# A hybrid decoder step on one core: the down projection's first 3584 rows as seven block products

## The chip, the cores and the metric

The kernel runs on one core of a Trainium2 chip. Its time is the device time of one execution in microseconds (us), and the number to predict is the median over runs. The engines are TensorE (PE, matmuls into PSUM), VectorE (DVE), ScalarE (ACT), GpSimd (POOL, which works on SBUF) and SyncE (SP, which here only issues DMAs). Each has its own queue of instructions that it takes in order; semaphores tie the queues together.

## The reference

1088 tokens (1024 of a prompt, 8 x 8 of samples), width 1024, one layer:

```python
h = rmsnorm(x, g_attn[i])
q, k, v, z, b_raw, a_raw, p, ga, gb = jnp.split(h @ w_in[i], offs, axis=-1)
...                                   # gated delta rule -> o_a; causal pooling -> o_b
merged = jax.nn.sigmoid(ga) * (o_a @ w_a_out[i]) + jax.nn.sigmoid(gb) * (o_b @ w_b_out[i])
x = x + merged @ w_o[i]
h2 = rmsnorm(x, g_mlp[i])
x = x + jnp.square(jax.nn.relu(h2 @ w_up[i])) @ w_down[i]
...
y = rmsnorm(x, g_final)
```

w_up is 1024 x 4096 and w_down 4096 x 1024. The rest of the outputs (states) are written before the part that the change touches. All is float32.

## The kernel before

**Layout and products.** Activations stand with channels on the 128 partitions and the 1088 tokens along the free axis (NT); a weight block of 128 x 128 is the stationary side of a matmul, tokens are the moving side. To keep float32 accuracy on a faster matmul type every operand is split into a hi part (a rounded copy, made by ACT) and a lo part (the rest, a subtraction of two SBUF tiles on DVE): `split`, lines 1045 and 1046. A product is three matmuls: hi x hi, hi x lo, lo x hi (lines 145 to 147, 1207).

**The stages around the change, in order.** `outs` merges the branches into tiles `mg`. `project(c)` runs for the two halves c of the tokens (CT = 544, each again cut in CB = 272): it multiplies by w_o, adds x, writes the new x (called x1) to DRAM (`x1_d`), sums squares into `acc` (ACT squares, POOL adds, L1126), and builds the seven token side operands of Strassen's algorithm for the up projection (`F`, L1132), split into `B[c]`. `norm2` turns `acc` into one over the norm: matmuls with ones (L1149), an inverse root on DVE (L89 to L94), transposes on PE (L82), a copy to `rb`. For c = 0 it is called in the second block of `project(1)`, for c = 1 after the first product of the up projection.

**The up projection** (`up_all`, `up_pair`) takes 16 pairs of 128 channels of w_up. A pair has seven products q (`product`, L1207), each 2 token halves x 4 blocks of depth x 3 matmuls of 272 columns, that is 168 matmuls. The weight operands of the next pair (`a_op`: sums on DVE into `S`, then a split) are made between the products, their loads (`a_raw`, L1169) a pair ahead. The products gather in three PSUM tiles b1, b2, b3 (out of four, `pp`): ACT copies partial sums out to SBUF (`copied`, L1224), DVE adds them (`plus`, L1236), `done` applies relu and the norm (DVE, L1230) and squares (ACT, L1231), and SP stores the result to DRAM (`h_d`, L1232).

**The down projection** (`down_all`) takes 8 groups of 512 rows of w_down. For 7 of them it loads h back (`acts`, L1287), splits it, and for each of 8 blocks of output channels and three stretches of tokens (384, 384, 320) makes 4 x 3 matmuls (`gemm`) into one PSUM tile, which DVE adds into x1 in SBUF (L1310). That is 288 matmuls a group. Weights are loaded and split per two output blocks (`weights`, L133, L134). The eighth group is done in `finish` with the tokens on partitions, together with the transposes of x1, the last norm and the output.

**Order.** The program text gives a priority; the scheduler of the tile framework lays out each engine's queue from it by a simulation, with tile slots handed out as they come free, and inserts the semaphores. A pool opened on memory that an older pool held makes its tiles wait for the older tiles that they overlap (`reuse_waits="tile"`). A tile of a ring (`big`, `bigy`, `tmp`, `wh`) waits in the same way for its predecessor's last reader.

Of the kernel before, what the change touches and what calls it, by code (L numbers as in the profile page):

```python
# [18 lines left out]
P = 128  # L19
# [50 lines left out]
class Builder:  # L70
    def __init__(self, tc, a, o):
        self.tc, self.nc, self.a, self.o = tc, tc.nc, a, o
        self.n, self.turn = 0, {}
# [129 lines left out]
    def build(self):  # L203
        tc, nc = self.tc, self.nc
        with ExitStack() as ctx, ExitStack() as ctx2:
# [12 lines left out]
            self.h_d = self.dp.tile([FF // P, P, NT], F32, name="h_d")  # L218
# [54 lines left out]
            ctxx.close()  # L273
            ctxy.close()
            self.pm = ctx.enter_context(tc.tile_pool(name="pm2", bufs=1, space=PSUM, reuse_waits="tile"))
            self.X = ctx.enter_context(tc.tile_pool(name="D", bufs=1, reuse_waits="tile"))
            self.nbig, self.mx = 27, self.X
            self.down_all()
# [4 lines left out]
    def bigy(self, dt=F32):  # L283
        return self.Y.tile([P, NT], dt, name=self.name("bigy"), tag="bigy", bufs=18)
# [778 lines left out]
    def outs(self):  # L1063
        nc, v = self.nc, self.nc.vector
        self.mg = [[tuple(self.bigy(F32R).rearrange("p (m t) -> p m t", m=2) for _ in range(2)) for _ in range(4)]
                   for _ in range(2)]
# [26 lines left out]
    def project(self, c):  # L1093
# [3 lines left out]
        ops = [tuple((self.big if c == 0 or q < 2 else self.bigy)(F32R).rearrange("p (k t) -> p k t", k=4)  # L1097
                     for _ in range(2)) for q in range(7)]
        self.B.append(ops)
        acc = self.st.tile([P, CT], F32, name=self.name("acc"), tag="acc", bufs=1)  # L1100
        cols = slice(c * CT, (c + 1) * CT)
        for i in range(KD):
# [10 lines left out]
            if i == 1 and c == 1:  # L1113
                self.norm2(0, self.acc)
# [24 lines left out]
        self.acc = acc  # L1139

    def norm2(self, c, acc):

        nc, v = self.nc, self.nc.vector
        ss = self.sm.tile([P, 6], F32, name=self.name("ss2"), tag="ms6", bufs=2)
        v.memset(ss, 1.0)
        ps = self.pp()[:, 0, :]
        cuts = [(b, j, min(P, CB - j * P)) for b in range(2) for j in range(3)]
        for n, (b, j, rows) in enumerate(cuts):
            nc.tensor.matmul(ps[0:rows, n:n + 1], lhsT=acc[:, b * CB + j * P:b * CB + j * P + rows],  # L1149
                             rhs=self.one, start=True, stop=True)  # L1150
        for n, (b, j, rows) in enumerate(cuts):
            v.tensor_scalar(out=ss[0:rows, n:n + 1], in0=ps[0:rows, n:n + 1], scalar1=1.0 / D, scalar2=EPS,
                            op0=ALU.mult, op1=ALU.add)
        rstd = self.rsqrt(ss, 6)
        ps = self.pp()
        for n, (b, j, rows) in enumerate(cuts):
            self.tr(ps[:, b, j * P:j * P + rows], rstd[0:rows, n:n + 1].broadcast_to([rows, P]), rows)
        nc.scalar.copy(out=self.halves(self.rb[:, c * CT:(c + 1) * CT]), in_=ps[:, :, 0:CB])


    def a_raw(self, i):

        if not hasattr(self, "raws"):
            self.raws, self.aops, self.ss_, self.na = {}, {}, {}, -1
        if i < 16 and i not in self.raws:
            tag = ("wr", "wl")[i % 2]
            self.raws[i] = [self.wp.tile([P, 4, 256], F32, name=self.name("raw"), tag=tag, bufs=2) for _ in range(2)]
            for j, t in enumerate(self.raws[i]):
                self.nc.sync.dma_start(out=t, in_=self.a["w_up"][0, j * 512:(j + 1) * 512, i * 256:(i + 1) * 256]  # L1169
                                       .rearrange("(k p) c -> p k c", p=P))  # L1170

    def a_op(self, i, q):
# [18 lines left out]
        self.na += 1  # L1191
        if self.na % 5 == 4:
            t = self.wp.tile([P, D], F32R, name=self.name("ao"), tag="wh", bufs=2)
        else:
            t = self.bigy(F32R)
# [14 lines left out]
    def up_pair(self, i, cs, side):  # L1210
# [11 lines left out]
        def copied(ps):  # L1222
            t = self.tmp()
            nc.scalar.copy(out=at(t), in_=ps[:, sl, 0:CB])  # L1224
            return t

        def done(src, t, row, n):

            rb = self.rb.rearrange("p (c n t) -> p n c t", c=2, n=2)[:, n, sl, :]
            v.scalar_tensor_tensor(out=at(t), in0=src, scalar=0.0, in1=rb, op0=ALU.max, op1=ALU.mult)  # L1230
            nc.scalar.activation(out=at(t), in_=at(t), func=AF.Square)  # L1231
            nc.sync.dma_start(out=self.h_d[2 * i + row].rearrange("p (c n t) -> p n c t", c=2, n=2)[:, n, sl, :],  # L1232
                              in_=at(t))
# [5 lines left out]
        c1 = copied(b1)  # L1239
# [18 lines left out]
        done(at(c16), c16, 0, 1)  # L1258
        side(5)
        run(6, b1, False)  # L1260
        h21 = self.tmp()
        done(b1[:, sl, 0:CB], h21, 1, 0)
        side(6)

    def up_all(self):
        def first(q):
            if q + 2 < 7:
                self.a_op(0, q + 2)
            if q == 0:
                self.norm2(1, self.acc)  # L1270
                self.a_raw(1)
        self.up_pair(0, (0,), first)
        self.up_pair(0, (1,), lambda q: self.a_op(1, q))
        for i in range(1, 16):
            def side(q):
                if q == 0:
                    self.a_raw(i + 1)
                self.a_op(i + 1, q)
            self.a_raw(i + 1)
# [3 lines left out]
    def acts(self, g):  # L1283
        out = []
        for f in range(4 * g, 4 * g + 4):
            raw = self.big()
            self.nc.sync.dma_start(out=raw, in_=self.h_d[f])  # L1287
            hi, lo = self.big(F32R), self.big(F32R)
            for n in range(2):
                s = slice(n * CT, (n + 1) * CT)  # L1290
                self.split(hi[:, s], lo[:, s], raw[:, s])
            out.append((hi, lo))
            yield out

    def down_all(self):
        v = self.nc.vector
        *_, acts = self.acts(0)
        self.x1 = []
        for m in range(KD):
            self.x1.append(self.big())  # L1300
            self.nc.sync.dma_start(out=self.x1[m], in_=self.x1_d[m])
        for g in range(7):
            nxt = self.acts(g + 1)
            for m in range(KD):
                if m % 2 == 0:
                    w = self.weights(self.a["w_down"][0, g * 512:(g + 1) * 512, m * P:(m + 2) * P], 4)
                for tb, (t0, n) in enumerate(TBS):
                    ps = self.gemm(w, m % 2, self.sub(acts), tb, 4)
                    x = self.x1[m][:, t0:t0 + n]
                    v.tensor_tensor(out=x, in0=x, in1=ps, op=ALU.add)  # L1310
                if m % 2 == 1:
                    new = next(nxt)
            acts = new
        self.finish(acts, 7 * 512)

    def finish(self, acts, row):
# [3 lines left out]
        for k in range(4):  # L1320
            raw = self.load(self.a["w_down"][0, row + k * P:row + (k + 1) * P, :], 1)
            hi, lo = (self.big(F32R), self.big(F32R)) if k < 4 - 3 else (None, None)
            w.append(self.weights(None, 1, raw=raw, hi=hi, lo=lo))
        gf = self.X.tile([P, D], F32, name="gf", tag="gf", bufs=1)
        nc.gpsimd.dma_start(out=gf, in_=self.a["g_final"].unsqueeze(0).broadcast_to([P, D]))
        xn = [self.X.tile([P, 3, D], F32, name=self.name("xn"), tag=t, bufs=1) for t in ("hi0", "lo0", "hi1")]
        for c in range(NCH):
            rows = P if c < 8 else 64
            tok = slice(c * P, c * P + rows)
            y = xn[c // 3][0:rows, c % 3, :]  # L1330
# [6 lines left out]
            for s in range(2):  # L1337
# [9 lines left out]
                junk = self.X.tile([P, 512], BF16, name=self.name("jf"), tag="lo2", bufs=1)  # L1347
# [35 lines left out]
```

## Time and profile before

| | |
|---|---|
| median of 3 runs | 1586.9 us (1586.44 to 1590.38) |
| profiled execution | 1586.38 us, span of its instructions 1584.6 us |
| mean granted TensorE clock | 0.985 of full |
| PE busy | 1532.2 us (97%), 10443 matmul records |
| DVE, ACT, POOL busy | 942.9, 520.1, 95.9 us |
| DMA | 171.16 MB, 108 GB/s over the span |

Times in the profile count from the first instruction. A busy time is the sum of an engine's instructions, overlaps counted once. Matmuls overlap each other, so the length of one matmul record (about 0.29 us for 272 columns) is more than the step from one to the next; paces have to be taken from events that repeat. "idle ... <-X" names what the engine waited for. [...]

### The profile page before, as it was taken

How to read it: one execution, taken by the hardware profiler on the slowest of the kernel's cores; microseconds unless marked ns; L12 is line 12 of the kernel's file. 1: busy time of each engine (PE TensorE's matmuls, PEld its weight loads, DVE VectorE, ACT ScalarE, POOL GpSimd, SP SyncE). 2: the span in 40 equal slices, each digit the busy share in tenths (PEclk: the TensorE clock that was granted, in tenths of full speed). 3: DMA queues.
4: the chain of work that ended last, by engine and by line, in shares of the span. 5: the costliest groups of instructions: out<-in, count | busy, mean ns of one | idle time of the engine just before them, and what ended most of it. 6: DMA issues, size and time to landing. Idle time of an engine off the chain costs nothing. (4 is left out here: it accounts for less than half of the span.)

```text
span 1584.6 us, 26354 instructions
## 1 busy us (share of the span) xinstructions
PE 1532.2 (97%) x10443; PEld 1485.2 (94%) x10443; DVE 942.9 (60%) x2197; ACT 520.1 (33%) x1103; POOL 95.9 (6%) x129
## 2 busy tenths in 40 slices
PE   6999999999999999999889999999989999999997
PEld 5989898998999999999889999999979999999986
DVE  7677768758664274656676555555545454444456
ACT  5342423413322133214454444444432222111123
POOL 3200000000000122002220000000000000000000
PEclk9999999999999999999898999999989999999999
DMA  6431422232223434444443333332255323222212
GB/s 221 137 98 49 117 77 71 90 90 72 79 86 105 129 88 138 137 132 157 145 151 103 103 110 110 103 101 93 83 184 202 108 97 101 92 69 96 82 41 74
DMA packets 173541, 171.16 MB, mean 108 GB/s; under 512 B 19924, under 2 KB 155837, under 8 KB 173409
## 3 DMA queue, kind: packets, MB, share of 16 engines
q1 hardware_dynamic: 168137, 157.24, 31.3%
q0 software_dynamic: 4080, 12.13, 2.3%
q8 instruction: 82, 1.34, 0.4%
q14 instruction: 42, 0.34, 0.1%
q10 hardware_dynamic: 1200, 0.10, 0.1%
HBM read 118.73 MB, written 50.83 MB: 107 GB/s over the span
## 5 line engine op out<-in xcount | busy, mean ns | idle before, releaser
L145 PE MATMUL pm<-big,wh 128*128 128x384 f32 (+1 forms) x864 | 283.4, 329 | 6.9 <-ACT big L1045 6.9
L145 PE MATMUL pm<-hi,wh 128*128 128x384 f32 (+1 forms) x840 | 284.3, 339 | 0.1
L146 PE MATMUL pm<-lo,wh 128*128 128x384 f32 (+1 forms) x840 | 282.4, 336 | 1.3 <-DVE lo L425 1.3
L147 PE MATMUL pm<-big,wl 128*128 128x384 f32 (+1 forms) x864 | 283.6, 328 | 0.0
L146 PE MATMUL pm<-big,wh 128*128 128x384 f32 (+1 forms) x864 | 283.4, 328 | 0.0
L147 PE MATMUL pm<-hi,wl 128*128 128x384 f32 (+1 forms) x840 | 280.4, 334 | 0.0
L1207 PE MATMUL pp<-big,bigy 128*128 128x272 f32 x1392 | 189.4, 291 | 2.8 <-ACT bigy L1045 2.8
L133 ACT CAST wh<-wr 128x1024 fp32r<-128x1024 f32 x88 | 92.5, 1051 | 294.4 <-PE pm L146 241.5
L1207 PEld LDWEIGHTS pp<-big,bigy 128*128 128x128 f32 x1392 | 182.2, 192 | 3.2 <-ACT bigy L1045 2.9
L1310 DVE TENSOR_TENSOR big<-big,pm 128x384 f32<-128x384 f32 x168 | 88.9, 531 | 151.7 <-PE pm L147 151.7
L145 PEld LDWEIGHTS pm<-big,wh 128*128 128x128 f32 x864 | 163.1, 189 | 8.3 <-ACT big L1045 8.0
L147 PEld LDWEIGHTS pm<-big,wl 128*128 128x128 f32 x864 | 163.2, 189 | 0.0
L146 PEld LDWEIGHTS pm<-big,wh 128*128 128x128 f32 x864 | 163.1, 189 | 0.0
L146 PEld LDWEIGHTS pm<-lo,wh 128*128 128x128 f32 x840 | 159.6, 190 | 3.6 <-DVE lo L425 1.8
L145 PEld LDWEIGHTS pm<-hi,wh 128*128 128x128 f32 x840 | 159.2, 190 | 2.5 <-DVE hi L421 0.5
L147 PEld LDWEIGHTS pm<-hi,wl 128*128 128x128 f32 x840 | 159.5, 190 | 0.2
L134 DVE TENSOR_TENSOR wl<-wr,wh 128x1024 fp32r<-128x1024 f32 x88 | 107.7, 1224 | 65.7 <-ACT wh L133 62.4
L1207 PE MATMUL pp<-bigy,bigy 128*128 128x272 f32 x768 | 106.8, 288 | 0.0
L1207 PEld LDWEIGHTS pp<-bigy,bigy 128*128 128x128 f32 x768 | 100.3, 188 | 0.0
L147 PE MATMUL pp<-bigy,wl 128*128 128x272 f32 x256 | 74.6, 291 | 0.0
L145 PE MATMUL pp<-bigy,wh 128*128 128x272 f32 x256 | 74.4, 291 | 0.0
L146 PE MATMUL pp<-bigy,wh 128*128 128x272 f32 x256 | 74.2, 290 | 0.0
(341 smaller groups left out, 2256.0 us busy)
## 6 DMA issues: line engine op xcount, KB each, us to landing
big<-h_d SPq DMA_DIRECT2D x32, 544.0 KB
wr<-in_w_in_dram SPq DMA_DIRECT2D x33, 512.0 KB
raw<-in_w_up_dram SPq DMA_DIRECT2D x32, 512.0 KB
wr<-in_w_down_dram SPq DMA_DIRECT2D x32, 512.0 KB
h_d<-tmp SPq DMA_DIRECT2D x60, 272.0 KB
wr<-in_w_o_dram SPq DMA_DIRECT2D x16, 512.0 KB
tmp<-xT_d SPq DMA_DIRECT2D x16, 272.0 KB
x_d<-tmp POOLq DMA_DIRECT2D x16, 272.0 KB, 2.3
```

The source lines that it names most:

```text
L133: nc.scalar.copy(out=hi, in_=raw)
L134: (nc.gpsimd if early else nc.vector).tensor_tensor(out=lo, in0=raw, in1=hi.bitcast(F32), op=ALU.subtract)
L145: mm(ps, lhsT=wh, rhs=xh, start=first, stop=False)
L146: mm(ps, lhsT=wh, rhs=xl, start=False, stop=False)
L147: mm(ps, lhsT=wl, rhs=xh, start=False, stop=last)
L1207: mm(out, lhsT=l[:, k, :], rhs=r[:, k, :], start=first and k + n == 0, stop=k == 3 and n == 2, skip_group_check=not first)
L1310: v.tensor_tensor(out=x, in0=x, in1=ps, op=ALU.add)
```

## The change

The down projection of rows 0 to 3583 is made by the same algorithm of seven products. Seven token side operands per pair of up channels are stored (`F_d`) in place of h: three are results of `done` themselves, four are differences that POOL makes in the up projection (`less`). In the down projection each group of 512 rows has four steps (two token halves c, two halves pp of the output channels); a step has seven products of 2 x 2 x 3 matmuls of 272 columns. The weight side sums are made by POOL (`da_op`), x1 (`x1t`) is loaded by ACT's queue, and additions into x1 are shared by DVE (straight from PSUM) and POOL (from ACT's copies). The PSUM pool of the up projection stays in use. The last 512 rows are done in `finish` as before.

The pool `Y` is cut into `Ya` (10 tiles, stays) and `Yb` (8 tiles). `norm2` is cut in two calls three blocks or products apart. All weight operands of the up projection use `bigy` (before, one in five used a `wh` tile); the first partial sum of a pair and the first `acc` share a tile `tq`.

```diff
+            self.h_d = self.dp.tile([4, P, NT], F32, name="h_d")
+            self.F_d = self.dp.tile([14, 7, P, CT], F32, name="F_d")
...
+                ctxx.close()
+                ctxy.close()
+                self.X = ctx.enter_context(tc.tile_pool(name="D", bufs=1, reuse_waits="tile"))
+                self.nbig = 21
+                self.x1t = self.X.tile([P, KD, NT], F32, name="x1t")
+                for m in range(KD):
+                    nc.scalar.dma_start(out=self.x1t[:, m, :], in_=self.x1_d[m])
+                self.down_all()
...
-            if i == 1 and c == 1:
-                self.norm2(0, self.acc)
+            if c == 1 and i in (1, 4):
+                self.norm2(0, self.acc0, i == 4)
...  # in up_pair
+        def keep(t, q):
+            nc.sync.dma_start(out=self.F_d[i, q].rearrange("p (c t) -> p c t", c=2)[:, sl, :], in_=at(t))
+        def less(o, a, b, q):
+            nc.gpsimd.tensor_tensor(out=at(o), in0=at(a), in1=at(b), op=ALU.subtract)
+            keep(o, q)
...  # after product 5
+        if i < 14:
+            t2, t4 = (self.wp.tile([P, D], F32, name=self.name("t24"), tag="wh", bufs=2)[:, 0:CT] for _ in range(2))
+            less(c167, c16, c1, 3)
+            less(c16, c5, c16, 4)
+            less(t2, c5, c167, 2)
...  # after product 6
+        if i < 14:
+            less(t4, h21, t2, 6)
...  # in up_all
-                self.norm2(1, self.acc)
+            if q in (1, 4):
+                self.norm2(1, self.acc1, q == 4)
...
+    def da_op(self, g, pp, q):
...
+        for k in range(2):
+            a11, a12, a21, a22 = (quad(k, i, j) for i in range(2) for j in range(2))
+            if q == 2:
+                po.tensor_tensor(out=blk(S[0], k), in0=a21, in1=a22, op=ALU.add)
+                po.tensor_tensor(out=blk(S[1], k), in0=blk(S[0], k), in1=a11, op=ALU.subtract)
+            elif q == 4:
+                po.tensor_tensor(out=blk(S[2], k), in0=a11, in1=a21, op=ALU.subtract)
+            elif q == 5:
+                po.tensor_tensor(out=blk(S[1], k), in0=a12, in1=blk(S[1], k), op=ALU.subtract)
+            if q in (0, 1, 6):
+                self.split(blk(hi, k), blk(lo, k), {0: a11, 1: a12, 6: a22}[q])
+        if q not in (0, 1, 6):
+            self.split(hi, lo, {2: S[1], 3: S[0], 4: S[2], 5: S[1]}[q] if q >= 2 else None)
...
+    def db_load(self, g, c, q):
+        t = self.big(F32R)
+        hi, lo = (t[:, n * CT:(n + 1) * CT] for n in range(2))
+        self.nc.sync.dma_start(out=lo.bitcast(F32).rearrange("p (k t) -> p k t", k=2),
+                               in_=self.F_d[2 * g:2 * g + 2, q, :, c * CB:(c + 1) * CB].rearrange("k p t -> p k t"))
...
+    def db_op(self, g, c, q):
+        hi, lo = self.bops[g, c, q]
+        self.split(hi, lo, lo.bitcast(F32))
+    def down_step(self, g, c, pp, side):
+        b1, b2, b3 = (self.pp() for _ in range(3))
...  # run: for p in 2, k in 2, three matmuls of 272 columns; add(x, t, eng): x = x + t
+        run(0, b1, True)
+        c1 = copied(b1)
+        side(0)
+        run(1, b2, True)
+        add(xv(0, 0), b2[:, :, 0:CB], v)
+        add(xv(0, 0), c1, po)
+        side(1)
+        run(2, b1, False)
+        c16 = copied(b1)
+        side(2)
+        run(3, b3, True)
+        add(xv(1, 1), b3[:, :, 0:CB], v)
+        side(3)
+        run(4, b1, False)
+        c167 = copied(b1)
+        add(xv(1, 1), c167, po)
+        side(4)
+        run(5, b3, False)
+        add(xv(0, 1), b3[:, :, 0:CB], v)
+        add(xv(0, 1), c16, po)
+        side(5)
+        run(6, b1, False)
+        add(xv(1, 0), b1[:, :, 0:CB], v)
+        side(6)
...  # down_all: loads, splits and weight parts are placed by product number, up to 28 products ahead
```

## Rows read from the trace of the kernel before

**Rows 1.** The page: busy time of PE, and the chain that ended last by line.
```profile
PE 1532.2 (97%) x10443; PEld 1485.2 (94%) x10443; DVE 942.9 (60%) x2197; ACT 520.1 (33%) x1103; POOL 95.9 (6%) x129
...
PE pp L1207 21%; PE pm L145 7%; PE pm L147 7%; PE pm L146 7%; PE pm L1345 1%; PE pm L1344 1%; PE pm L1343 1%; PE pp L145 1%; PE pp L147 1%; PE pp L146 1%; PE pt L82 0%; DMA big<-h_d 0%; PE pp L82 0%; DVE F L1132 0%; DVE xn L1356 0%; ACT jf L1348 0%
```

**Rows 2.** Windows: length, busy us (count) by engine, PE clock, DMA, GB/s.
```profile
782.00:784.00 2.00, 0.00 (x0) 0.00 (x0) 2.00 (x11) 0.66 (x3) 2.00 (x1) 0.50 1.05 317
...
860.00:1174.00 314.00, 314.00 (x2510) 314.00 (x2510) 172.43 (x258) 130.21 (x219) 0.56 (x1) 1.00 0.30 101
1174.00:1192.00 18.00, 11.14 (x45) 9.74 (x44) 7.79 (x12) 6.88 (x11) 0.00 (x0) 0.72 0.95 352
1192.00:1519.00 327.00, 326.99 (x1983) 326.96 (x1983) 155.16 (x250) 62.66 (x85) 0.00 (x0) 1.00 0.29 98
```

**Rows 3.** Timeline of SP's queue, up projection: start, length, engine, line, what.
```profile
1041.86 3.50 SPq L1169 DMA_DIRECT2D raw<-in_w_up_dram  x2
...
1083.92 3.50 SPq L1169 DMA_DIRECT2D raw<-in_w_up_dram  x2
```

**Rows 4.** Timeline of SP's queue, down projection, 15 weight loads left out between.
```profile
1283.63 0.37 SPq L116 DMA_DIRECT2D wr<-in_w_down_dram  x1
...
1473.71 0.34 SPq L116 DMA_DIRECT2D wr<-in_w_down_dram  x1
```

**Rows 5.** Timeline of PE at the two calls of norm2.
```profile
785.66 1.71 PE L82 MATMUL pp<-ident,rs 128*128 128x128 f32 x6 [6.85 <-DVE rs L94]
787.30 0.59 PE L145 MATMUL pp<-bigy,wh 128*128 128x272 f32 x1
...
790.16 0.28 PE L145 MATMUL pp<-bigy,wh 128*128 128x272 f32 x1
...
828.61 1.41 PE L1149 MATMUL pp<-one,acc 128*128 128x1 f32 x12 [2.13 <-POOL acc L1126]
832.78 3.39 PE L1207 MATMUL pp<-big,bigy 128*128 128x272 f32 x12 [2.77 <-ACT bigy L1045]
```

**Rows 6.** Timeline of all engines between the up and the down projection, PE's rows.
```profile
1179.98 1.24 PE L145 MATMUL pm<-big,wh 128*128 128x384 f32 x2 [4.87 <-ACT big L1045]
...
1185.28 1.50 PE L145 MATMUL pm<-big,wh 128*128 128x384 f32 x3 [1.99 <-ACT big L1045]
```

**Rows 7.** The chain that ended last, in order of time: start, length, what.
```profile
839.46 335.67 PE pp L1207 x2660
...
1519.00 0.87 PE pt L82 x8
```

**Rows 8.** Groups by shape, 860 to 1174 us: busy, mean ns, idle before.
```profile
L1046 DVE TENSOR_TENSOR bigy<-S,bigy 128x512 fp32r<-128x512 f32 x45 | 31.1, 692 | 47.8 <-ACT bigy L1045 47.8
...
L1236 DVE TENSOR_TENSOR tmp<-tmp,pp 128x544 f32<-128x544 f32 x30 | 21.6, 720 | 24.6 <-PE pp L1207 24.6
...
L1224 ACT COPY tmp<-pp 128x544 f32<-128x544 f32 x60 | 36.8, 613 | 86.6 <-issue 53.8 <-PE pp L1207 32.9
```

**Rows 9.** Groups by shape, 1174 to 1585 us.
```profile
L1046 DVE TENSOR_TENSOR big<-big,big 128x544 fp32r<-128x544 f32 x64 | 44.5, 720 | 21.0 <-ACT big L1045 21.0
...
L1045 ACT CAST big<-big 128x544 fp32r<-128x544 f32 x64 | 38.7, 645 | 106.8 <-PE pm L146 56.0 <-DMA big<-h_d 50.0 <-DVE big L1310 0.7
```

**Rows 10.** Timeline of POOL, two stretches.
```profile
11.12 2.33 POOL L134 TENSOR_TENSOR wl<-raw,wh 128x1024 fp32r<-128x1024 f32 x1 [10.67 <-DVE rstd L107]
...
780.89 4.61 POOL L1126 TENSOR_TENSOR acc<-acc,tmp 128x544 f32<-128x544 f32 x1 [1.56 <-ACT tmp L1125]
...
797.17 1.45 POOL L1126 TENSOR_TENSOR acc<-acc,tmp 128x544 f32<-128x544 f32 x1 [0.69 <-ACT tmp L1125]
...
827.23 1.32 POOL L1126 TENSOR_TENSOR acc<-acc,tmp 128x544 f32<-128x544 f32 x1 [0.63 <-ACT tmp L1125]
```

**Rows 11.** Timeline of DVE beside the POOL add at 797.17.
```profile
796.95 0.43 DVE L1132 TENSOR_TENSOR F<-F 128x272 f32<-128x272 f32 x1
797.35 1.56 DVE L1046 TENSOR_TENSOR big<-F,big 128x272 fp32r<-128x272 f32 x1
```

More of the change, by code (lines that the diff above doesn't have):

```diff
@@ L1138, in project, with norm2 @@
                     self.split(ops[q][0][:, kt, :], ops[q][1][:, kt, :], F[:, s, :])
-        self.acc = acc
-    def norm2(self, c, acc):
+        if c == 0:
+            self.acc0 = acc
+        else:
+            self.acc1 = acc
+    def norm2(self, c, acc, second):
         nc, v = self.nc, self.nc.vector
-        ss = self.sm.tile([P, 6], F32, name=self.name("ss2"), tag="ms6", bufs=2)
-        v.memset(ss, 1.0)
-        ps = self.pp()[:, 0, :]
         cuts = [(b, j, min(P, CB - j * P)) for b in range(2) for j in range(3)]
[L1148 to L1154, printed above, removed]
+        if not second:
+            ss = self.sm.tile([P, 6], F32, name=self.name("ss2"), tag="ms6", bufs=2)
+            v.memset(ss, 1.0)
+            ps = self.pp()[:, 0, :]
+            for n, (b, j, rows) in enumerate(cuts):
+                nc.tensor.matmul(ps[0:rows, n:n + 1], lhsT=acc[:, b * CB + j * P:b * CB + j * P + rows],
+                                 rhs=self.one, start=True, stop=True)
+            for n, (b, j, rows) in enumerate(cuts):
+                v.tensor_scalar(out=ss[0:rows, n:n + 1], in0=ps[0:rows, n:n + 1], scalar1=1.0 / D, scalar2=EPS,
+                                op0=ALU.mult, op1=ALU.add)
+            self.rstd2 = self.rsqrt(ss, 6)
+            return
         ps = self.pp()
         for n, (b, j, rows) in enumerate(cuts):
-            self.tr(ps[:, b, j * P:j * P + rows], rstd[0:rows, n:n + 1].broadcast_to([rows, P]), rows)
+            self.tr(ps[:, b, j * P:j * P + rows], self.rstd2[0:rows, n:n + 1].broadcast_to([rows, P]), rows)
         nc.scalar.copy(out=self.halves(self.rb[:, c * CT:(c + 1) * CT]), in_=ps[:, :, 0:CB])
@@ L1277, in side @@
                     self.a_raw(i + 1)
-                self.a_op(i + 1, q)
-            self.a_raw(i + 1)
-            self.up_pair(i, (0, 1), side)
[L1283 to L1287, printed above, removed]
+                if i < 15:
+                    self.a_op(i + 1, q)
+                    if i == 14 and q == 3:
+                        self.da_raw(0, 0)
+                else:
+                    self.da_op(0, 0, q)
@@ new lines, in db_load, with run, copied, add @@
+    def db_load(self, g, c, q):
[3 more added lines that the diff above has]
+                               in_=self.F_d[2 * g:2 * g + 2, q, :, c * CB:(c + 1) * CB].rearrange("k p t -> p k t"))
+        self.bops[g, c, q] = hi, lo
+    def db_op(self, g, c, q):
+        hi, lo = self.bops[g, c, q]
+        self.split(hi, lo, lo.bitcast(F32))
+    def down_step(self, g, c, pp, side):
+        nc, v = self.nc, self.nc.vector
+        b1, b2, b3 = (self.pp() for _ in range(3))
+        xq = self.x1t.rearrange("q (pp p i) (c n t) -> q pp i c n p t", p=2, i=2, c=2, n=2)
+        xv = lambda i, n: xq[:, pp, i, c, n]
+        def run(q, ps, first):
+            ah, al = self.aops[g, pp, q]
+            bh, bl = (t.rearrange("p (k t) -> p k t", k=2) for t in self.bops[g, c, q])
+            for p in range(2):
+                for k in range(2):
+                    for n, (l, r) in enumerate(((ah, bh), (ah, bl), (al, bh))):
+                        nc.tensor.matmul(ps[:, p, 0:CB], lhsT=l[:, k, p, :], rhs=r[:, k, :], start=first and k + n == 0,
+                                         stop=k == 1 and n == 2, skip_group_check=not first)
+        def copied(ps):
+            t = self.halves(self.tmp())
+            nc.scalar.copy(out=t, in_=ps[:, :, 0:CB])
+            return t
+        def add(x, t, eng):
+            eng.tensor_tensor(out=x, in0=x, in1=t, op=ALU.add)
+        po = nc.gpsimd
+        run(0, b1, True)
[22 more added lines that the diff above has]
+        side(6)
@@ new lines, in down_all, with side @@
+    def down_all(self):
+        nc = self.nc
+        self.bops = {}
+        G = 7
+        ev = [[] for _ in range(28 * G + 40)]
+        for g in range(G):
+            for q in range(7):
+                for c in range(2):
+                    t = 28 * g + 14 * c - 14 + 2 * q
+                    ev[max(t, 0)].append(lambda g=g, c=c, q=q: self.db_load(g, c, q))
+                    ev[max(t + 3, 0)].append(lambda g=g, c=c, q=q: self.db_op(g, c, q))
+            for n in range(14):
+                pp, q = n // 7, n % 7
+                t = 28 * g - 14 + int(1.4 * n)
+                if q == 0 and (g or pp):
+                    ev[max(t - 8, 0)].append(lambda g=g, pp=pp: self.da_raw(g, pp))
+                if g or pp:
+                    ev[max(t, 0)].append(lambda g=g, pp=pp, q=q: self.da_op(g, pp, q))
+        self.last = []
+        for f in range(4):
+            ev[28 * G - 12 + 2 * f].append(lambda f=f: self.last_act(f, False))
+            ev[28 * G - 9 + 2 * f].append(lambda f=f: self.last_act(f, True))
+        first = ev[0]
+        for e in first[:]:
+            e()
+        ev[0] = []
+        t = 0
+        for g in range(G):
+            for c, pp in ((0, 0), (0, 1), (1, 1), (1, 0)):
+                def side(q):
+                    for e in ev[t + q + 1]:
+                        e()
+                    ev[t + q + 1] = []
+                self.down_step(g, c, pp, side)
+                t += 7
+        for e in ev:
+            for f in e:
+                f()
@@ L1288, in acts, with last_act @@
+    def last_act(self, f, second):
+        if not second:
             hi, lo = self.big(F32R), self.big(F32R)
+            self.nc.sync.dma_start(out=lo.bitcast(F32), in_=self.h_d[f])
+            self.last.append((hi, lo))
+        else:
+            hi, lo = self.last[f]
             for n in range(2):
                 s = slice(n * CT, (n + 1) * CT)
[L1291 to L1314, printed above, removed]
@@ L1329, in finish @@
             tok = slice(c * P, c * P + rows)
-            y = xn[c // 3][0:rows, c % 3, :]
+            y = self.big()[0:rows, 0:D]
             for s in range(2):
```

81 lines of the change are left out of this document (50 added, 31 removed).

## The prediction

> **What bounds the kernel now.** I read the busy shares and the chain by line first [rows 1]: TensorE (PE) is busy for 97% of the span, and the chain that ended last is almost only its matmuls, L1207 (the up projection's products) and L145 to L147 (every other product, the down projection's among them). So a change pays if it takes matmul time away without putting another engine's wait in its place. The windows by stage come next [rows 2]: from 860 to 1174 us (up) and from 1192 to 1519 us (down) PE has no idle time and full clock, while VectorE (DVE) works 172 of 314 us in the one and 155 of 327 us in the other, ScalarE (ACT) 130 and 63, GpSimd (POOL) nothing. Between the two stages, at 1174 to 1192, PE is busy for 11 of 18 us at a granted clock of 0.72.
>
> The pace of a matmul is read from issues that repeat once per block of work, since a busy PE record is longer than the step to the next one. In the up projection the weight loads repeat every (1083.92 - 1041.86) / 2 = 21.03 us [rows 3], and a pair there is 7 x 2 x 12 = 168 matmuls of 272 columns: 125.2 ns each. In the down projection the sixteenth weight load after that at 1283.63 is at 1473.71 [rows 4]: 11.88 us for 72 matmuls of 384, 384 and 320 columns, 165.0 ns each.
>
> **The steady down projection, on PE.** Removed: 7 groups x 288 = 2016 matmuls x 165.0 = 332.6 us. Added: 7 groups x 4 steps x 7 products x 12 = 2352 matmuls of 272 columns. That is the shape of the up projection, 128 x 128 weights included, so 125.2 ns each: 294.5 us, 10.52 us a step and 1.50 us a product. If nothing else is late, 38.1 us go.
>
> **What the other engines do beside it, per group of 42.1 us.** Durations: ACT copies 544 elements out of PSUM in 0.613 us, DVE adds 544 from PSUM in 0.720, and a 512-element lo part takes 0.69 [rows 8]; a 544-element lo part takes 0.720, its hi part on ACT 0.645 [rows 9]. POOL takes 2.33 us for 1024 and 1.32 for 544 [rows 10], 2.1 ns an element, so I estimate 0.72 us for 256.
> - DVE: 16 adds from PSUM x 0.72 = 11.5; 14 token lo parts x 0.72 = 10.1; weight lo parts 8 x 0.69 and 12 halves of 256 at about 0.41 (272 take 0.43 [rows 11]) = 10.4. Sum 32.0 of 42.1.
> - ACT: 12 copies x 0.613, 14 hi parts x 0.645, 8 x 0.62 (estimate beside the 0.645) and 12 x 0.4: 26 of 42.1.
> - POOL: 12 adds x 1.32 = 15.8 and 16 weight sums x 0.72 = 11.5: 27.3 of 42.1.
> Each fits by itself. DVE and POOL don't run side by side, though. At 797.17 POOL starts an add of two SBUF tiles; the DVE subtraction issued at 797.35 takes 1.56 us, where its neighbour of the same size takes 0.43, and ends 0.29 us after POOL does [rows 10, 11]. The other way round, a POOL add that met an unbroken run of DVE work (782 to 784 us) [rows 2] took 4.61 us [rows 10]. So a DVE instruction with two SBUF inputs and a POOL add exclude each other. The lo parts are of that kind: 20.5 us of DVE's 32.0. Upper bound by whole durations: 20.5 + 27.3 = 47.8 us a group, 12.0 a step. Lower bound, counting only what seems to exclude (0.14 less for each of 34 DVE instructions, since 0.43 - 0.29 lay before POOL's end, and 0.08 less for each of 28 POOL ones, whose add at 797.17 lost 1.45 - 1.32 = 0.13 to a subtraction that ran 0.21 into it): 40.8, or 10.2 a step. PE's 10.52 lies between.
>
> Where would lateness reach PE first? b3 is written by product 3, added into x1 by DVE, and accumulated into by product 5: one product, 1.50 us, is all the time DVE has. A lo part ahead of it that waits for a POOL sum makes 0.72 + 0.72 + 0.72 = 2.2 us, behind a POOL add 2.8: PE then waits 0.7 to 1.3 us. I take such a wait in about half of the steps, 0.45 us a step, since POOL is in an instruction for two thirds of the time. The copies that free b1 are ACT's and have the same 1.50 us; 0.645 + 0.613 fits. So 28 x 10.97 = 307.2 us instead of 332.6: **-25.4 us**; the ends are -38.1 (all hidden) and 28 x 12.0 = 336, +3.4.
>
> **The change of stage.** Before, PE's first down product starts at 1179.98 and stalls again until 1185.28, both times for hi parts of h on ACT, which waits for the loads [rows 6]. From the end of the up projection's last matmul, 839.46 + 335.67 = 1175.1, to the first transpose behind the down projection at 1519.0 it takes 343.9 us [rows 7], 11.2 above the steady 332.6. After, the weights of group 0 are prepared during the last pair, but the sums still wait for memory that the up projection holds, then a load, a hi and a lo part: again about 5 us, and then some us at half clock, as after the stall at 785 us, where twelve matmuls took 2.86 us [rows 5]. Eight loads of x1 (4.5 MB) move to ACT's queue, in front of its hi parts, and share the DMA engines with the sums. At the 352 GB/s of that stretch [rows 2] they and the first sums take some 18 us, but the first add needs only two slices, and the four PSUM tiles let PE run a step ahead. I take 8 us in place of 11.2: **-3**, ends -11 (no stall) and +5.
>
> **The norm in two parts.** [...] With the transposes three blocks later, all of that is covered by matmuls: 6.85 + 0.8 + 1.36 = **-9.0 us** (ends -6.9 and -9.5). For the second half of the tokens the wait of 2.13 us for POOL at 828.61 goes behind another product [rows 5]; the wait for weight parts at 832.78 stays, since it comes from DVE's chain, which is some 2 us shorter now: **-2.5** (0 to -6).
>
> **The up projection's additions.** 14 pairs get four POOL subtractions (4 x 1.32 = 5.3 us) and seven stores of 278 KB in place of four. POOL was empty. DVE's work with two SBUF inputs is 4 x 0.72 + 11 x 0.69 = 10.5 us of a pair (`done`, a `plus`, 7 lo parts, 4 sums), so the two together need 15.8 of 21.03. The deadlines are one product of 24 matmuls, 3 us. SP's queue gets three more issues a pair behind POOL's results; the weight loads that could be stuck there are issued a whole pair ahead [rows 3]. **+1** (0 to +7).
>
> **The end.** The last products start only when PSUM has been handed to another pool, behind DVE's last add of 0.72 us; 1.5 us (0 to 4). The first transposes read token columns that were finished half a group earlier.
>
> Sum, against the profiled execution's 1586.4 us (span 1584.6 and 1.8 around it; the median of three runs is 1586.9): 1586.4 - 25.4 - 3 - 9.0 - 2.5 + 1 + 1.5 = **1549 us**.
>
> [...]
>
> **Rivals.**
> 1. *The exclusion sets the pace.* Whole durations exclude: 12.0 us a step, 336 us, so the gain on PE is spent on DVE and POOL taking turns; the total is 1549 + 336 - 307 = 1578, and about 1567 if a step takes 11.6. For it: the rows at 797. Against it: DVE's adds read PSUM, 11.5 us a group in which POOL may run.
> 2. *All is hidden.* 10.52 us a step: 1549 - 12.7 = 1536. For it: the lower bound of the exclusion, 10.2 us, is under it, and x1 and the sums have a step of lead. Against it: DVE would have to be free within 1.50 us of product 3 in every one of 28 steps, with POOL in an instruction for two thirds of the time.
> 3. *POOL starves: slower.* Its adds free the tiles that ACT copies b1 into. If two of three adds a step are stretched to 4.61 us, POOL needs 6.9 + 2 x 3.3 = 13.5 us a step, five such tiles hold less than two steps, and PE waits in front of products 2 and 4: 378 us, total 1620. It decides from about 12.5 us a step on. For it: the one row at 780.89. Against it: DVE ran there without a gap, and it has about 2.5 us of slack a step here.
>
> **How the numbers follow.** Forecast (1540 to 1560): 0.48. Rival 1 (1560 to 1584): 0.24. Rival 2 (1525 to 1540): 0.18. Rival 3: 0.10. The range for 8 in 10 drops rival 3 and parts of the outer ends: 1530 to 1578. The runs shown lie within 0.25% of each other, so 0.3% (4.8 us) is about what can be told from no change: faster 0.86; the same 0.05, the top of rival 1 and the bottom of rival 3; slower 0.09.
>
> **What would show it.** In the profile after: 272-column matmuls at a pace of 125 ns in both stages; some 307 us of down projection; PE's waits in it put down to DVE's add into x1 (product 5), or, under rival 1 and 3, to ACT's copies and to weight parts; DVE lo parts and POOL adds far above 0.72 and 1.32 us; no wait for the inverse root near 785. I am wrong if a step of 84 matmuls takes under 10.6 us or over 11.4, or if the handover costs more than 15 us.

## The result, and the profile after

The changed kernel takes 1615.9 us (median of 4 runs, 1614.25 to 1618.35) against 1588.1 us for the kernel before beside it: a ratio of 1.0175, 95% interval 1.0155 to 1.0195. It is slower; the forecast was 1549 us. The profiled execution took 1618.35 us, its span 1616.2.

The page's line of busy times answers to [rows 1]:

```profile
PE 1510.3 (93%) x10779; PEld 1458.1 (90%) x10779; DVE 1071.3 (66%) x2295; ACT 620.8 (38%) x1341; POOL 422.2 (26%) x385
```

PE is busy for 21.9 us less than before, as wanted, yet the span is 31.6 us longer: PE now stands idle. The timeline of PE shows where the down projection begins and ends, beside [rows 6, 7] (start, length, what, idle time before it and its releaser). The three rows are the last products of the up projection, the first of the down projection and the first transposes behind it.

```profile
1167.94 1.67 PE L1218 MATMUL pp<-bigy,bigy 128*128 128x272 f32 x12
...
1187.28 8.52 PE L1377 MATMUL pp<-big,bigy 128*128 128x272 f32 x48 [17.67 <-ACT big L1054]
...
1550.73 1.03 PE L82 MATMUL pt<-ident,x1t 128*128 128x128 f32 x8
```

The change of stage costs 17.7 us, and the 28 steps take 1550.7 - 1187.3 = 363.5 us, 12.98 each, where the forecast had 10.97 and the matmuls alone need 10.52. The tail, 1616.2 - 1550.7 = 65.5 us, is what it was (65.6). The windows of the two stages answer to [rows 2] (length, busy us and count of PE, PEld, DVE, ACT, POOL, then PE clock, DMA, GB/s):

```profile
1174.00:1192.00 18.00, 4.72 (x20) 4.46 (x21) 4.61 (x8) 4.85 (x10) 0.00 (x0) 0.53 1.04 394
1200.00:1250.00 50.00, 41.28 (x309) 40.41 (x308) 43.98 (x56) 25.37 (x51) 34.18 (x27) 0.93 0.46 142
1250.00:1300.00 50.00, 44.14 (x348) 43.26 (x347) 40.28 (x50) 23.61 (x47) 36.60 (x32) 1.00 0.40 121
...
1450.00:1500.00 50.00, 42.05 (x318) 41.37 (x316) 32.49 (x44) 19.71 (x38) 27.52 (x24) 0.93 0.34 104
```

No engine is full: PE loses 5 to 9 of every 50 us in the steps, and DVE and POOL have room too. That points not to the amount of work on an engine but to a chain from one to the next; the experiments below test it. PE's own waits name its end (us in total, times, longest):

```profile
PE pp L1377 <- DVE x1t L1386: 25.6, 14, 5.2
PE pp L1377 <- ACT tmp L1382: 23.6, 14, 5.4
PE pp L1377 <- ACT big L1054: 17.7, 1, 17.7
```

Two things stretch, seen in the groups by shape from 1220 to 1530 us; DVE's first, beside the 720 and 692 ns of [rows 8, 9], then POOL's, beside the 1.32 us of [rows 10]:

```profile
L1055 DVE TENSOR_TENSOR big<-big 128x544 fp32r<-128x544 f32 x80 | 82.1, 1045 | 12.4 <-ACT big L1054 12.3
L1386 DVE TENSOR_TENSOR x1t<-x1t,pp 128x544 f32<-128x544 f32 x97 | 69.0, 714 | 38.9 <-PE pp L1377 38.4 <-issue 0.3
L1055 DVE TENSOR_TENSOR bigy<-raw,bigy 128x256 fp32r<-128x256 f32 x42 | 30.4, 756 | 5.3 <-ACT bigy L1054 5.2
L1055 DVE TENSOR_TENSOR bigy<-S,bigy 128x512 fp32r<-128x512 f32 x29 | 29.2, 1013 | 6.1 <-ACT bigy L1054 6.1
```
```profile
L1386 POOL TENSOR_TENSOR x1t<-x1t,tmp 128x544 f32<-128x544 f32 x73 | 113.7, 1563 | 99.6 <-DVE x1t L1386 62.0 <-ACT tmp L1382 32.5 <-ACT bigy L1054 3.0
L1343 POOL TENSOR_TENSOR S<-S,raw 128x256 f32<-128x256 f32 x22 | 20.8, 961 | 0.1
```

DVE's lo parts, with two SBUF inputs, went from 720 to 1045 ns, and so did POOL's additions (1.32 to 1.56 us). DVE's additions of the same size, with one input in PSUM, kept their 714. How that reaches PE is seen in one stretch of the timeline:

```profile
1325.03 2.42 POOL L1345 TENSOR_TENSOR S<-raw 128x256 f32<-128x256 f32 x2
...
1327.48 0.62 ACT L1054 CAST bigy<-S 128x512 fp32r<-128x512 f32 x1 [2.06 <-POOL S L1345]
1328.13 1.23 DVE L1055 TENSOR_TENSOR bigy<-S,bigy 128x512 fp32r<-128x512 f32 x1 [1.28 <-ACT bigy L1054]
...
1329.28 0.71 DVE L1386 TENSOR_TENSOR x1t<-x1t,pp 128x544 f32<-128x544 f32 x1
1329.37 0.60 ACT L1382 COPY tmp<-pp 128x544 f32<-128x544 f32 x1
...
1330.05 3.13 PE L1377 MATMUL pp<-big,bigy 128*128 128x272 f32 x23 [2.70 <-DVE x1t L1386]
```

ACT's hi part waits 2.06 us for POOL's sums, with ACT's next copy queued behind it; DVE's lo part waits for the hi part and then runs 1.23 us instead of 0.69, with DVE's addition queued behind it; PE waits 2.70 us for that addition. Each stretched instruction is passed on through three in-order queues.

### The profile page after: what moved, and what is told of

It reads as the page before. It is cut to its first block, busy times and chain, and to the rows that moved or that the text cites. A ratio compares the mean times of both kernels' runs of the same rounds, so it can differ in the third digit from the quotient of the medians.

```text
span 1616.2 us, 28150 instructions
## 1 busy us (share of the span) xinstructions
PE 1510.3 (93%) x10779; PEld 1458.1 (90%) x10779; DVE 1071.3 (66%) x2295; ACT 620.8 (38%) x1341; POOL 422.2 (26%) x385
## 4 chain that ended last, share of the span: by engine, by line
PE 76%; DVE 10%; DMA 6%; issue 3%; ACT 2%; POOL 2%; SPq 0%; ACTq 0%; DVEq 0%; POOLq 0%
PE pp L1218 20%; PE pm L146 10%; PE pp L1377 10%; PE pm L145 10%; PE pm L147 10%; DVE big L1055 3%; DMA big<-F_d 2%; PE pp L147 2%; PE pp L145 2%; PE pp L146 2%; PE pt L82 2%; PE pt L739 2%; DMA qk<-g_d 2%; DVE bigy L1055 2%; DVE x1t L1386 1%
## 5 line engine op out<-in xcount | busy, mean ns | idle before, releaser
L1377 PE MATMUL pp<-big,bigy 128*128 128x272 f32 x1440 | 194.7, 295 | 47.8 <-ACT tmp L1382 18.8
L1377 PEld LDWEIGHTS pp<-big,bigy 128*128 128x128 f32 x1440 | 188.7, 195 | 52.2 <-ACT tmp L1382 21.0
L1218 PE MATMUL pp<-big,bigy 128*128 128x272 f32 x1728 | 230.5, 289 | 3.2 <-ACT bigy L1054 3.2
L1218 PEld LDWEIGHTS pp<-big,bigy 128*128 128x128 f32 x1728 | 222.9, 189 | 3.3 <-ACT bigy L1054 3.3
L1386 POOL TENSOR_TENSOR x1t<-x1t,tmp 128x544 f32<-128x544 f32 x84 | 131.7, 1574 | 113.0 <-DVE x1t L1386 66.7
L1377 PE MATMUL pp<-big,big 128*128 128x272 f32 x912 | 124.9, 296 | 19.3 <-DVE x1t L1386 14.4
L1377 PEld LDWEIGHTS pp<-big,big 128*128 128x128 f32 x912 | 120.1, 195 | 22.4 <-DVE x1t L1386 16.1
L1055 DVE TENSOR_TENSOR big<-big 128x544 fp32r<-128x544 f32 x98 | 99.1, 1033 | 29.3 <-ACT big L1054 29.1
L1386 DVE TENSOR_TENSOR x1t<-x1t,pp 128x544 f32<-128x544 f32 x112 | 79.7, 714 | 48.0 <-PE pp L1377 47.5
L1218 PE MATMUL pp<-bigyb,bigy 128*128 128x272 f32 x768 | 106.6, 288 | 0.0
L1055 DVE TENSOR_TENSOR bigy<-raw,bigy 128x256 fp32r<-128x256 f32 (+1 forms) x100 | 81.1, 831 | 36.6 <-ACT bigy L1054 36.5
L1218 PEld LDWEIGHTS pp<-bigyb,bigy 128*128 128x128 f32 x768 | 100.2, 188 | 0.0
```

The lines of the kernel that those rows point to most:

```text
L1055: (eng or self.nc.vector).tensor_tensor(out=lo, in0=f, in1=hi.bitcast(F32), op=ALU.subtract)
L1218: mm(out, lhsT=l[:, k, :], rhs=r[:, k, :], start=first and k + n == 0, stop=k == 3 and n == 2, skip_group_check=not first)
L1377: nc.tensor.matmul(ps[:, p, 0:CB], lhsT=l[:, k, p, :], rhs=r[:, k, :], start=first and k + n == 0, stop=k == 1 and n == 2, skip_group_chec ...
L1386: eng.tensor_tensor(out=x, in0=x, in1=t, op=ALU.add)
```

## Experiments

Theory 1 is that chain: DVE's and POOL's SBUF inputs exclude each other, and in-order queues carry the delay to PE. Theory 2 is the order of the queues without the exclusion: additions and copies stand behind hi and lo parts that wait for POOL's sums. Theory 3 is that late loads of the token sums hold ACT up. Other rivals were that some engine simply has too much to do, or that the change of stage is what costs.

**No exclusion, POOL as busy.**

```diff
-                po.tensor_tensor(out=blk(S[0], k), in0=a21, in1=a22, op=ALU.add)
...
+                po.memset(blk(S[i], k), 0.0)
...
+            if eng is nc.gpsimd:
+                eng.memset(x, 0.0)
+                eng.memset(t, 0.0)
+                eng.memset(t[:, :, 0:100], 0.0)
```

> Every POOL addition of the down projection is replaced by memsets of about the same length on the same outputs (x1, the copy, the sums), so POOL is as busy and as late as before, and what waits for POOL still waits, but POOL reads no SBUF; the sums and additions themselves are left out of the result. Theory 1 (DVE and POOL exclude each other, and stretched lo parts make PE late): DVE's 544-element lo parts go back from 1.05 to about 0.72 us, a step from 13.0 to 10.6 to 11.2 us, total 1550 to 1570. Theory 2 (queue order: adds and copies stand behind hi and lo parts that wait for POOL's sums): the lo parts go back but PE still waits some 35 us or more, total 1590 to 1605. Theory 3 (ACT held up by late loads of the token sums): hardly faster, 1605 to 1616.

It took 1553.42 us, in one execution. The groups of DVE and of POOL from 1220 to 1480 us, one fence each:

```profile
L1388 DVE TENSOR_TENSOR x1t<-x1t,pp 128x544 f32<-128x544 f32 x97 | 69.6, 718 | 41.7 <-PE pp L1374 40.9
L1055 DVE TENSOR_TENSOR big<-big 128x544 fp32r<-128x544 f32 x74 | 52.5, 722 | 17.0 <-ACT big L1054 16.7
```
```profile
L1384 POOL MEMSET x1t<- 128x544 f32 x73 | 40.5, 554 | 36.0 <-DVE x1t L1388 35.9
L1385 POOL MEMSET tmp<- 128x544 f32 x72 | 39.9, 554 | 63.9 <-ACT tmp L1379 63.7
L1386 POOL MEMSET tmp<- 128x200 f32 x72 | 19.2, 266 | 3.1
```

POOL's three writes last 0.554 + 0.554 + 0.266 = 1.37 us, about as long as an undisturbed addition (1.32), in the same place in the queue and behind the same semaphores, but read nothing. The lo parts are back at 722 ns, PE's waits in the steps fall from 49 to 8 us, and the down projection, from 1177.19 to 1486.08, takes 308.9 us in place of 363.5. So it isn't POOL's speed or its semaphores, which theory 2 would need; it is what it reads.

**Half of POOL's work left out**, the weight sums or the additions:

```diff
-                po.tensor_tensor(out=blk(S[0], k), in0=a21, in1=a22, op=ALU.add)
...
-            self.split(hi, lo, {2: S[1], 3: S[0], 4: S[2], 5: S[1]}[q] if q >= 2 else None)
+            self.split(hi, lo, r[q % 2][:, q // 4, :])
```

> POOL's weight sums in the down projection are left out (the weight parts are split from loaded rows instead); POOL keeps its additions into x1. Theory 1: what excludes falls by 11.5 of 48 us a group, so 1575 to 1590. Theory 2: nothing on ACT or DVE waits for POOL's sums any more, PE's waits nearly go: 1555 to 1575. Theory 3: 1605 to 1616.

```diff
-            eng.tensor_tensor(out=x, in0=x, in1=t, op=ALU.add)
+            if eng is not nc.gpsimd:
+                eng.tensor_tensor(out=x, in0=x, in1=t, op=ALU.add)
```

> POOL's additions into x1 are left out (ACT still copies, DVE still adds from PSUM); POOL keeps the weight sums. Theory 1: what excludes falls by 15.8 of 48 us a group: 1565 to 1585. Theory 2: the sums are no longer behind additions in POOL's queue, but the chain of sum, hi part, lo part stays: 1580 to 1600. Theory 3: 1605 to 1616.

1575.77 and 1574.72 us, one execution each, with 544-element lo parts of 957 and 812 ns. The first time lies on the border of theories 1 and 2 and doesn't decide between them; PE's waits do, since 21.3 us of them stay in the steps though nothing waits for sums any more (19.8 us without the additions). Each half taken away gives some 40 us of the 62 that both give: the loss doesn't add up by halves, either half alone still costs some 22.

**POOL's work done by DVE**, all of it, and the additions alone:

```diff
-        nc, v, po = self.nc, self.nc.vector, self.nc.gpsimd
+        nc, v, po = self.nc, self.nc.vector, self.nc.vector
...
-        po = nc.gpsimd
+        po = nc.vector
```

> The changed kernel with one thing changed: POOL's weight sums and its additions into x1 of the down projection are issued on DVE, everything else (x1's loads on ACT's queue too) as in the change. Theory 1 (DVE and POOL exclude each other, and the lost time chains through the in-order queues): without any POOL work there is nothing to exclude; the down projection from its first product to the first transpose falls from 363.5 to 296 to 310 us, a 544-element lo part on DVE is back at 0.72 us instead of 1.05, and the time is 1543 to 1555 us; the wait of about 17 us at the change of stage stays, since x1's loads stay where they were. Rival (DVE's room is the bound: by whole durations it gets 47.2 us of work in a group of 42.1, 11.8 us a step): 28 x 11.8 = 330 us, 1580 us. Rival (the wait at the change of stage is what costs): hardly faster than 1606.

> The changed kernel with POOL's additions into x1 (three a step, 15.8 us a group) issued on DVE, the weight sums (16 a group, 11.5 us) still on POOL; x1's loads on ACT's queue as in the change. Theory 1: the exclusion stays for the sums, and DVE has 12 more instructions a group that need it; lo parts of 544 elements stay stretched (0.8 to 1.0 us), PE waits more for DVE's additions, and the time is 1565 to 1600 us, above the version with all of it on DVE. Rival (POOL is too slow at the additions that free the copies' tiles, and the sums are harmless): as good as with all of it on DVE, 1543 to 1555 us, lo parts at 0.72 us.

With everything on DVE: 1550.28 us (1548.55 to 1550.6), ratio to before 0.9764 [0.9747, 0.978]. With the sums left on POOL: 1580.95 (1579.37 to 1585.36), 0.9966 [0.9953, 0.9979], lo parts at 803 ns. Both times came where theory 1 had them, and their difference, 30.7 us, is what the sums alone cost on POOL. With them there PE waits 8.3 us for DVE's additions and 15.9 for ACT's copies in the steps. PE's waits and three rows of its timeline, everything on DVE:

```profile
PE pp L1377 <- ACT big L1054: 16.2, 1, 16.2
PE pp L1377 <- ACT tmp L1382: 3.4, 5, 1.2
```
```profile
1163.02 1.67 PE L1218 MATMUL pp<-bigy,bigy 128*128 128x272 f32 x12
1180.89 18.25 PE L1377 MATMUL pp<-big,bigy 128*128 128x272 f32 x120 [16.20 <-ACT big L1054]
...
1483.26 1.03 PE L82 MATMUL pt<-ident,x1t 128*128 128x128 f32 x8
```

The steps take 302.4 us, and 544-element lo parts 0.73. Adding 15.2 us a group to DVE's 32.0 made the kernel 65.6 us faster. By whole durations DVE has 47.2 us of work in a group of 42.1 (rival: 1580); its timeline shows why it fits:

```profile
1324.57 0.72 DVE L1055 TENSOR_TENSOR big<-big 128x544 fp32r<-128x544 f32 x1
1325.21 0.72 DVE L1386 TENSOR_TENSOR x1t<-x1t,tmp 128x544 f32<-128x544 f32 x1
1325.84 0.72 DVE L1386 TENSOR_TENSOR x1t<-x1t,pp 128x544 f32<-128x544 f32 x1
1326.47 0.72 DVE L1055 TENSOR_TENSOR big<-big 128x544 fp32r<-128x544 f32 x1
```

Neighbours start 0.63 us apart, 0.09 less than one lasts. With 78 instructions a group (28 additions, 14 token and 20 weight lo parts, 16 sums) that takes an estimated 7 us off the 47.2, which leaves less than PE's 42.1.

**x1's loads behind the first sums.**

```diff
-                for m in range(KD):
-                    nc.scalar.dma_start(out=self.x1t[:, m, :], in_=self.x1_d[m])
...
+        for m in (0, 2, 1, 3, 4, 6, 5, 7):
+            nc.sync.dma_start(out=self.x1t[:, m, :], in_=self.x1_d[m])
```

> Same work; the eight loads of x1 go to SP's queue, behind the first loads of token sums, instead of to ACT's queue ahead of ACT's first hi part. If these loads made the handover of 17.7 us (they fill the DMA engines and ACT's queue), PE's first wait falls to 5 to 8 us and the total to 1602 to 1608; the steps stay at 13 us. If the wait is for memory that the up projection holds, it stays at 15 to 18 us and the total at 1612 to 1618.

1606.84 us (1605.39 to 1608.29), ratio 1.012 [1.009, 1.0149]. PE's waits:

```profile
PE pp L1375 <- DVE x1t L1384: 24.0, 13, 4.5
PE pp L1375 <- ACT tmp L1380: 23.0, 11, 5.4
PE pp L1375 <- ACT big L1052: 9.2, 1, 9.2
```

The first wait falls from 17.7 to 9.2 us, not quite to the 5 to 8 expected; the time is in its range. The others stay: the two losses are separate. In the changed kernel ACT's queue stands in these loads until its first hi part:

```profile
1170.86 15.68 ACTq L281 DMA_DIRECT2D x1t<-x_d  x7
...
1172.12 15.17 SPq L1357 DMA_DIRECT2D big<-F_d  x10
1186.58 2.83 ACT L1054 CAST big<-big 128x544 fp32r<-128x544 f32 x5 [15.10 <-DMA big<-F_d]
```

Whether the queue or the 4.5 MB that they move at the same time does more of it, this run doesn't separate; it takes both away. The rows lean to the queue: the last issue ends at 1186.54, and five hi parts start at 1186.58, back to back. Each of the eight issues takes only some 0.33 us; what spreads them over 16 us isn't shown.

**Both together**: x1's loads behind, everything on DVE.

> x1_behind with POOL's sums and additions given to DVE, so that nothing in the down projection excludes anything; DVE's work is 32.0 + 12 x 0.72 + 16 x 0.41 = 47.2 us a group by whole durations, more than PE's 42.1. Theory 1 (exclusion): DVE at its own rate sets the pace, 11.2 to 11.9 us a step, the down projection at 315 to 335 us from PE's first product on, total 1560 to 1580, faster than x1_behind (1607) though DVE has a quarter more to do. Theory 2 (queue order): adds and copies stand behind even more DVE work, 1595 or more.

1536.75 us (1535.86 to 1537.63), ratio 0.968 [0.9644, 0.9717]: faster than both kernels and than its expectation. Two windows show PE and DVE both almost full:

```profile
1200.00:1250.00 50.00, 49.34 (x393) 48.90 (x392) 48.74 (x91) 27.72 (x56) 0.00 (x0) 1.00 0.36 106
1250.00:1300.00 50.00, 50.00 (x402) 49.89 (x401) 49.55 (x97) 27.52 (x54) 0.00 (x0) 1.00 0.49 154
```

Of PE's waits there only 8.2 us at the change of stage remain, and 1.7 us in the steps.

**Fewer hands, POOL keeping the sums**: x1's loads behind, ACT's copies and POOL's additions replaced by DVE additions straight from PSUM.

```diff
-        c1 = copied(b1)
+        add(xv(0, 0), b1[:, :, 0:CB], v)
...
-        add(xv(0, 0), c1, po)
```

> x1_behind with DVE adding every partial sum straight from PSUM (seven adds a step in place of four, no copies by ACT, no additions by POOL); POOL keeps the weight sums. Theory 1: excluding work is 20.5 + 11.5 = 32.0 us a group, but DVE has 40.7 us of its own and is blocked for part of POOL's 11.5, so 11.5 to 12.5 us a step, total 1575 to 1600. Theory 2: ACT's copies, behind which PE waited, are gone, so 1560 to 1575.

1560.28 us (1557.27 to 1563.29), 0.9828 [0.9786, 0.9871]: 23.5 us above the version with everything on DVE. It is a miss for theory 1, which had 1575 to 1600, and at the lower end of theory 2's range. Lo parts take 776 ns, and PE waits 14.0 us for DVE's additions. How much of the gain over 1606.84 is the copies' isn't separated. The run without POOL's additions kept the copies, and with x1's loads behind it would come to some 1566 us (1574.72 less 9, an estimate), so most of it seems to be POOL's additions.

**Another order**: each product summed over the seven groups in PSUM, 56 additions in place of 196, nothing on POOL, weight sums kept in DRAM, x1's loads behind.

```diff
-        b1, b2, b3 = (self.pp() for _ in range(3))
+        ps = self.pp()
+        for g in range(7):
+            ah, al = self.aops[q, pp, g]
+            bh, bl = (t.rearrange("p (k t) -> p k t", k=2) for t in self.bops[q, c, g])
```

> Another order of the same 2352 matmuls: each of the seven products is summed over all seven groups of 512 rows in one PSUM tile before it is added into x1. That takes 56 additions in place of 196, all by DVE, and POOL is not used in the down projection; the weight sums are made once by DVE, kept in DRAM and read back; loads and stores grow to some 75 MB. DVE: 56 x 0.72 + 98 x 0.72 + 98 x 0.69 + 56 x 0.69 = 217 us beside 294.5 of matmuls. Theory 1: no exclusion, nothing late but the start: down projection 300 to 310 us, total 1535 to 1550. If the DMA engines (512-byte pieces, 255 GB/s) or ACT's queue behind late loads (theory 3) hold PE up, 1560 or more.

1572.34 us (1571.04 to 1574.33), 0.9902 [0.9873, 0.9931]: a miss. Windows, in the order used above:

```profile
1200.00:1250.00 50.00, 50.00 (x404) 50.00 (x403) 36.32 (x57) 18.66 (x30) 0.00 (x0) 1.00 0.82 249
1250.00:1300.00 50.00, 30.54 (x186) 28.64 (x186) 25.75 (x39) 7.54 (x12) 0.00 (x0) 0.76 0.85 273
1300.00:1350.00 50.00, 42.31 (x297) 40.98 (x296) 37.45 (x58) 24.57 (x39) 0.00 (x0) 0.90 0.91 303
1350.00:1400.00 50.00, 50.00 (x405) 50.00 (x404) 30.75 (x47) 18.85 (x31) 0.00 (x0) 1.00 0.57 185
```

The loss lies in one place, the third product, whose weight parts each need three loads and three stores: there DVE's sums wait for their loads, at 0.85 to 0.91 of the DMA engines' time. In the other windows shown PE is full.

**The norm alone**: the kernel before with `norm2` in two calls and nothing else.

```diff
-            if i == 1 and c == 1:
-                self.norm2(0, self.acc)
+            if c == 1 and i in (1, 4):
+                self.norm2(0, self.acc, i == 4)
```

> The kernel before with norm2 alone cut in two calls three blocks or products apart, as in the change; the down projection is the old one. By the prediction's term this takes 9.0 + 2.5 us away: 1575 to 1579 beside 1587. If something else stands in the way at the same place (DVE's own queue), 1582 to 1587.

1575.81 us (1573.9 to 1577.06), 0.9925 [0.99, 0.9951], 10.8 us less than before. Its last up products, behind the same row of the kernel before, one fence each:

```profile
1173.43 1.67 PE L1207 MATMUL pp<-bigy,bigy 128*128 128x272 f32 x12
```
```profile
1161.88 1.67 PE L1209 MATMUL pp<-bigy,bigy 128*128 128x272 f32 x12
```

## Why the prediction was wrong, step by step

From 1586.4 to 1618.35 us, by the two profiled executions: end of the up projection -5.5 (1175.1 to 1169.6), change of stage +6.4 (11.2 to 17.6), steps +30.9 (332.6 to 363.5), the rest +0.2.

- **The steady down projection failed**: -25.4 forecast, +30.9 measured. PE's side holds: with x1's loads behind and everything on DVE the steps take 300.2 us (1170.14 to 1470.35), 1.7 of it waits, beside 294.5 of matmuls. What failed is "such a wait in about half of the steps, 0.45 us a step": the steps lose 2.46 us each (12.98 - 10.52). PE's waits in them are 28, with 1.76 us on average and up to 5.4, in place of 14 of 0.7 to 1.3. Half of this is a term that the prediction put at nothing, the copies of ACT ("0.645 + 0.613 fits"): 23.6 us, beside 25.6 for DVE's additions. Without exclusion the copies cost 7.9.

  The prediction saw the exclusion [rows 10, 11] and the short deadline, and then priced one late instruction. Its upper bound, 12.0 by whole durations, was none: it supposed that an engine kept waiting by the other finds work when it is let go. In in-order queues it often doesn't: between 1220 and 1530 us DVE waits 38.4 us for PE ahead of its additions, POOL 62.0 for DVE and 32.5 for ACT ahead of its own. That the run without exclusion, 308.9 us, comes near the forecast's 307.2 is luck: the forecast's 12.7 us above the matmuls were for the exclusion.

  Of the 69 us above the matmuls' 294.5, 49 are waits named above. For the other 20 the rows show granted clocks of 0.93 to 0.97 in six of seven windows of 50 us between 1200 and 1550, which PE didn't have before [rows 2]. Added up they fall short of full clock by 0.26 x 50 = 13 us, an estimate of what that cost; the rest isn't separated. Even without these 13 a step takes 12.5 us, more than the bound.
- **The rivals.** Rival 3 (1620 us, "decides from about 12.5 us a step on") had the time, and given 0.10 it was priced too low. Its way was not quite this: it wanted POOL short of time, its additions at 4.61 us. POOL's additions take 1.56 us, and it is busy for 24 to 37 of 50 us. Rival 1 took whole durations for the worst; rival 2's time, 1536, is that of the kernel with x1's loads behind and everything on DVE.
- **The change of stage** was mis-sized: 8 us forecast in place of 11.2, and it came to 17.6, which is +6.4, beyond the upper end of +5. The prediction had x1's loads on ACT's queue in view, and thought that PE could start on two slices. ACT's hi parts could not: 8.5 of the 17.7 us went with the loads' place.
- **The norm** was right: -9.0 and -2.5, and the norm alone moved the last up products by 11.55 us. Of the three terms of the 9.0, [rows 5] show the wait of 6.85 us and the twelve matmuls in 2.86 us, 1.36 above 1.50. No run shows the 0.8: from the six transposes to the next matmul it took 1.64 us before (785.66 to 787.30) and 0.99 in the profile after, behind matmuls (805.22 to 806.21), 0.65 less. In the profiled execution after, little of this is seen, since it ran late already in code that the change doesn't touch. From 460 to 480 us PE's granted clock was 0.83 there and 1.00 before. The two windows, after and then before:

```profile
460.00:480.00 20.00, 19.77 (x192) 17.54 (x192) 11.57 (x30) 4.09 (x15) 0.00 (x0) 0.83 0.03 11
```
```profile
460.00:480.00 20.00, 19.78 (x151) 17.50 (x150) 13.94 (x45) 5.81 (x19) 1.95 (x3) 1.00 0.26 75
```

  The up projection of the changed kernel ended, where PE's wait ahead of the first down product begins, at 1169.61 us there (1187.28 - 17.67), and between 1161.76 (no exclusion) and 1167.04 (x1's loads behind) in the profiles of eight experiments with the same code up to then. The one window doesn't explain the order: the latest of the eight, with x1's loads behind, had 1.00 in it, and one that ended at 1161.94, both together, had 0.97 from 450 to 500, beside 0.93 after. What made the executions differ stays open.
- **The up projection's additions**, +1 forecast: from 924.20 to 1092.46, two equal weight loads eight pairs apart, a pair takes 21.03 us, as before [rows 3]. They cost nothing, though POOL and DVE meet there too. From 860 to 1160 us DVE's lo parts that meet POOL's subtractions take 1001 ns, beside the 692 of [rows 8], and PE is busy for 300.00 of 300 us:

```profile
L1055 DVE TENSOR_TENSOR bigy<-raw,bigy 128x512 fp32r<-128x512 f32 x41 | 41.0, 1001 | 26.3 <-ACT bigy L1054 26.2
```

  So stretching alone doesn't cost time. That DVE is less loaded there (176 of 300 us) and that a product has 3 us would be the reason; no run tests it.
- **The end**, +1.5: no wait shows; the last products run into the transposes at 1550.73.

The signs asked for were there: no wait for the inverse root, PE waiting for DVE's addition into x1, lo parts far above 0.72 us. The step of 12.98 us and the 17.7 us at the change of stage are both past what the prediction named as its failure.

## What to carry to other kernels

Before giving POOL a share of work beside DVE, count DVE's instructions with two SBUF inputs in the same stretch (here these took 1045 ns beside POOL's additions in place of 720, while additions of the same size from PSUM kept 714): if they are frequent, try the same work on DVE first, even where DVE looks full by busy time. The stretching itself was there in the up projection too and cost nothing (1001 ns in place of 692, a pair still took 21.03 us); look at what waits for the stretched instruction, and how soon. Where instructions exclude each other and feed each other through in-order queues, the sum of whole durations is no upper bound (a step took 12.98 us, with a sum of 12.0); one product of slack (1.5 us) is less than two stretched instructions in a row (2 x 1.045). And loads put on the queue of an engine that computes stand in front of its next instructions: here ACT's first hi part started at 1186.58 us, right behind the last of them (1186.54).

## What the runs showed of the hardware

- POOL's reading was what excluded here: 1.37 us of POOL as writes left DVE's subtractions of two SBUF tiles at 722 ns; POOL's additions made 1045 of them and took 1.56 us themselves, 1.32 undisturbed. DVE's additions of the same size with one input in PSUM took 714 ns beside POOL's additions and 718 beside its writes.
- DVE's back-to-back instructions of 544 elements start 0.63 us apart while each is recorded at 0.72, so that a DVE busy for 49.6 of 50 us kept up with PE though its work adds up to 47.2 us in 42.1.
- The same code up to the end of the up projection ran up to 7.9 us apart between nine profiled executions (1161.76 to 1169.61 us at that end), with the granted clock at 0.83 in one window of the latest.
